# Feed-forward products by one level of a Strassen-type algorithm, in slots of half a product

## The chip, the cores and the metric

One core of a Trainium2 chip runs the kernel. The time is device microseconds of one execution, and the median of three runs is given. The core's engines work side by side and wait for each other by semaphores: TensorE (PE, matmuls into the banks of PSUM; its weight loads are PEld), VectorE (DVE), ScalarE (ACT), GpSimd (POOL) and SyncE (SP, which issues most loads and stores).

## What is computed

Two blocks follow each other on 1024 tokens of width 1024: the first has a gated linear attention and a pooling branch, the second has attention heads of two kinds and then a feed-forward part. The change is in the feed-forward part. All arithmetic is float32.

```python
x = x + o @ w_out[l]
h = rmsnorm_2(x, ffn_norm_g[l])
u = causal_dwconv(h @ w_up[l], conv_w[l], conv_b[l])   # three taps along the tokens
gate, val = jnp.split(u, 2, axis=-1)                   # 2816 columns each
x = x + (jax.nn.silu(gate) * val) @ w_down[l]
return rmsnorm_2(x, final_norm_g)
```

## The kernel before

Activations lie with features on the 128 partitions and 1024 tokens along the row, so x is 8 tiles, u is 44 tiles (22 gate, 22 value) and the feed-forward activations are NFF = 22 tiles. A product is exact to float32 by splitting both sides in two float32r parts, hi and lo, and doing three matmuls for one (`mm3`, lines 236 to 238: `ah*bl`, `al*bh`, `ah*bh`). A matmul is 128x128 weights against 512 tokens, one bank of PSUM. `gemm` does one tile of output columns, for the two halves of the tokens, over its k tiles.

Weights come in by `load` (line 227): a DMA of 256 KB on SP's queue to `wraw`, a cast on ScalarE to `whi` and a subtraction on GpSimd to `wlo`:

```python
nc.scalar.copy(hi, src)
tt(lo, src, hi.bitcast(F32), ALU.subtract, eng)   # eng is GpSimd, or VectorE if None
```

`tt` is a tensor_tensor operation (line 182), `stt` a scalar_tensor_tensor (line 185), both on VectorE if no engine is named.

The feed-forward part begins in the output projection of attention. For each of the 8 tiles of x2 (lines 1113 to 1126) VectorE scales the two halves out of PSUM (`t<-lg,rs`) and adds them (`x<-x,t`), ScalarE squares, GpSimd (for the last tile VectorE) adds the squares to `acc`, and the tile times the norm's weights is split to `u3h` (ScalarE) and `u3l` (VectorE). The first up product uses the first six tiles before the sums of squares are taken (`gemm_late`, line 1128). The factor of the norm, R3, is multiplied in as a product leaves PSUM (line 1143).

Then for each of 22 feed-forward tiles: an up product and convolution for the gate tile and the value tile (`conv`: one pass on ScalarE, two taps of `stt` on VectorE), a sigmoid, two products on VectorE, a split to `fh` and `fl`. For each two of them, `down` multiplies with the rows of w_down and adds to x2 out of PSUM (`x<-x,pp`). The order is that of the program as the framework's scheduler lays it out, and each next group's up products are traced ahead of the down products. The last two tiles and the final norm are done for some tokens at a time.

Tiles of the main pool are 32 slots of 1040 values, those of the weights 2 raw, 4 hi and 4 lo.

Of the kernel before, what the change touches and what calls it, by code (L numbers as in the profile page):

```python
# [9 lines left out]
F32 = mybir.dt.float32  # L10
# [7 lines left out]
P = 128  # L18
# [40 lines left out]
# columns of the vector table (one value per partition and column)  # L59
# [11 lines left out]
# columns of the constant table  # L71
# [7 lines left out]
# the first column tile of each block of w_mod  # L79
# [16 lines left out]
def fused_blocks(ctx, tc, io, out, dbg=None):  # L96
# [11 lines left out]
    wpool = ctx.enter_context(tc.tile_pool(name="wpool", bufs=1))  # L108
    sb = ctx.enter_context(tc.tile_pool(name="sb", bufs=1))
# [8 lines left out]

    def ld(name):
# [10 lines left out]
    def ht(name, dt=F32):  # L130
        return sb.tile([P, HALF], dt, tag="h", bufs=NH, name=f"{name}_{uid()}")
# [16 lines left out]
    # ---- constants  # L148
# [31 lines left out]
    # ---- arithmetic helpers  # L180
    def tt(o, a, b, op, eng=None):
        return (eng or nc.vector).tensor_tensor(out=o, in0=a, in1=b, op=op)  # L182

    def stt(o, a, s, b, op0, op1, eng=None):
        return (eng or nc.vector).scalar_tensor_tensor(out=o, in0=a, scalar=s, in1=b, op0=op0, op1=op1)  # L185

    def split(src, hi, lo, eng=None, scale=None):
        """src (times scale, one value per partition) = hi + lo exactly, both in float32r."""
        if scale is None:
            nc.scalar.copy(hi, src)  # L190
            tt(lo, src, hi.bitcast(F32), ALU.subtract, eng)
        else:
            nc.scalar.activation(hi, src, AF.Copy, scale=scale)
# [10 lines left out]
    def log_exp_table(after):  # L204
        """Loads the table that has both functions, past the last use of another."""
# [3 lines left out]
    def rstd(total, r, n, scale=1.0 / D):  # L209
        """r = 1 / sqrt(total * scale + eps): exp(-ln / 2), then one Newton step."""  # L210
# [9 lines left out]
    def sigmoid(src, o):  # L220
        """o = 1 / (1 + exp(-src)) as exp(-ln(1 + exp(-src)))."""
# [4 lines left out]
    # ---- products: weights are split into two float32r parts as they come in  # L226
# [15 lines left out]
    def gemm(parts, xh, xl, ranges=XH, c=P, c0=0, m=P, per=4, ks=range(KD), tag="pp"):  # L242
        """A tile of output columns; gives a bank of PSUM for each range of tokens."""
# [24 lines left out]
    def bank_rstd(acc, r, scale=1.0 / D, tag="pp"):  # L268
        """r = 1 / sqrt(mean + eps) from sums over all partitions of acc [128, 1024]."""
# [7 lines left out]
    def need(key):  # L277
        """Emits fillers up to the one called key."""
# [3 lines left out]
    def weave(fill, chain):  # L282
        """Emits each filler (key, step, function) before the given step of the chain."""
# [23 lines left out]
    x1_d = [dtile(f"x1_d{k}") for k in range(KD)]  # L307
    ra_d = dtile("ra_d")
# [7 lines left out]
    # ================================================================== block 1  # L316
# [3 lines left out]
    # conditioning vectors through silu  # L320
# [8 lines left out]
    # x and ctx (features first) and their norms  # L329
# [12 lines left out]
    # shift, scale (and later gate): the products with w_mod, 512 columns at a time, four tiles of  # L342
    # features side by side on the array; a second product sums the four and turns them to columns
# [63 lines left out]
    for b in range(2):  # L407
# [9 lines left out]
        for k in range(4 * b, 4 * b + 4):  # L417
# [4 lines left out]
            hl.append(b1k(f"hl{k}", F32R))  # L422
# [26 lines left out]
        # the gate inputs as [hi; lo; hi] on 96 partitions  # L449
# [30 lines left out]
    def proj_v(h):  # L480
        """v, token-major."""
# [16 lines left out]
    def proj_z(n, ct):  # L498
        """silu of the z parts, the sigmoid of the g parts, u itself."""
# [10 lines left out]
    # ---- gated linear attention of one head; yields between its steps  # L510
    def gla_head(h):
# [7 lines left out]
        # running sums of the log decays in each chunk (the 1/16 goes into the exponentials):  # L519
        # X[i] is the sum of the first i of the chunk  # L520
# [23 lines left out]
        # scores [key, query] of each chunk, by levels of halving: at each level the decays are  # L544
        # taken from the middle of the block, so that no exponent is above zero
# [60 lines left out]
        # queries against the states, decayed keys that build them  # L606
# [62 lines left out]
        # outputs, normed over the head  # L669
# [30 lines left out]
    def pool_tile(gi, i):  # L700
        """One tile of the pooled differences, in float32r parts."""
# [6 lines left out]
        # doubled window sums: s_w[t] covers t - w/2 .. t + w/2 - 1  # L708
# [71 lines left out]
    # branch products and the merge  # L780
# [17 lines left out]
    for ct in range(KD):  # L798
        sg, m = ld("sg"), b1k("mB")
# [26 lines left out]
    # residual; the two norms that follow it share their reads  # L826
    uh, ul = [], []
    accA, accB = b1k("accA"), b1k("accB")
    for ct in range(KD):
# [14 lines left out]
        ul.append(b1k("ul", F32R))  # L844
# [52 lines left out]
    def proj_v2(p):  # L897
        """v of two heads, turned to token-major."""
# [10 lines left out]
    def proj_f():  # L909
        """The running sums of the log forget gates, as rows [1, 1, F, -F, 1, 1] in parts."""  # L910
# [440 lines left out]
```

## Time and profile before

| | us |
|---|---|
| median of three runs | 2675.65 |
| lowest and highest run | 2673.03, 2675.9 |
| span of the profiled execution, first to last instruction | 2679.3 |

| engine | busy us | share of the span | instructions |
|---|---|---|---|
| PE | 2549.1 | 95% | 14390 |
| PEld | 2015.2 | 75% | 14390 |
| DVE | 1505.9 | 56% | 2190 |
| ACT | 961.0 | 36% | 1634 |
| POOL | 809.5 | 30% | 592 |

The profiled execution has no time of its own beside its span. Shares are means over all stages. Busy time of an engine holds the time in which an instruction that was begun could not go on. Matmuls overlap in their pipeline, so the mean duration of one is longer than their spacing; the spacing is a stretch of time divided by the matmuls in it.

### The profile page before, as it was taken

To read this page: it belongs to the slowest core of one execution; us is meant where nothing else is said; L and a number is where in the kernel's file an instruction comes from. 1 tells how busy PE (TensorE), PEld (TensorE's weight loads), DVE (VectorE), ACT (ScalarE), POOL (GpSimd) and SP (SyncE) were. 2 spreads that over 40 slices of the span, in tenths; PEclk is the share of its full clock that TensorE was granted. 3 is DMA by queue.
4 is the path that set the end of the run, shared out by engine and by line. 5 is a ranking of instruction groups with operands and counts; after the bars stand their busy time and mean duration, and the time that the engine had idled before them with its cause. 6 is when DMAs were issued, how large, how long until landed. Compare 5 with 4: busy or idle time off the path is not lost. (4 is left out here: it accounts for less than half of the span.)

```text
span 2679.3 us, 36279 instructions
## 1 busy us (share of the span) xinstructions
PE 2549.1 (95%) x14390; PEld 2015.2 (75%) x14390; DVE 1505.9 (56%) x2190; ACT 961.0 (36%) x1634; POOL 809.5 (30%) x592
## 2 busy tenths in 40 slices
PE   6989999999999999999999999999899999999996
PEld 3878977777787888876777766666688888888885
DVE  6363292765927223255766677788934444444456
ACT  4342262553734412332333443433422222222233
POOL 1432221221212224434233222233433333333334
PEclk9989999999999999999999999999999999999998
DMA  6423242433424553335444323430111111111112
GB/s 256 125 74 108 86 158 85 151 111 101 145 80 146 196 193 110 118 103 155 127 127 127 113 77 114 124 105 28 40 49 49 48 48 48 47 48 48 48 48 75
DMA packets 109113, 270.55 MB, mean 101 GB/s; under 512 B 13600, under 2 KB 18592, under 8 KB 108944
## 3 DMA queue, kind: packets, MB, share of 16 engines
q1 hardware_dynamic: 101648, 244.90, 28.3%
q0 software_dynamic: 7296, 23.34, 3.7%
q8 instruction: 113, 1.85, 0.3%
q14 instruction: 56, 0.46, 0.1%
HBM read 192.40 MB, written 71.57 MB: 99 GB/s over the span
## 5 line engine op out<-in xcount | busy, mean ns | idle before, releaser
L182 POOL TENSOR_TENSOR wlo<-wraw,whi 128x512 fp32r<-128x512 f32 (+1 forms) x363 | 537.3, 1482 | 1639.2 <-ACT whi L190 1593.1
L190 ACT CAST whi<-wraw 128x512 fp32r<-128x512 f32 (+1 forms) x363 | 223.8, 617 | 709.4 <-PE pp L238 617.6
L236 PE MATMUL pp<-hl,whi 128*128 128x512 f32 (+1 forms) x768 | 312.1, 407 | 4.8 <-DVE hl L185 4.8
L237 PE MATMUL pp<-hh,wlo 128*128 128x512 f32 (+1 forms) x768 | 307.2, 400 | 0.4 <-POOL wlo L182 0.4
L238 PE MATMUL pp<-hh,whi 128*128 128x512 f32 (+1 forms) x768 | 306.4, 399 | 0.0
L238 PE MATMUL pp<-u3h,whi 128*128 128x512 f32 x688 | 271.4, 395 | 0.0
L237 PE MATMUL pp<-u3h,wlo 128*128 128x512 f32 x688 | 271.0, 394 | 0.0
L236 PE MATMUL pp<-u3l,whi 128*128 128x512 f32 x688 | 270.2, 393 | 0.0
L182 DVE TENSOR_TENSOR x<-x,pp 128x512 f32<-128x512 f32 (+1 forms) x184 | 121.5, 664 | 208.5 <-PE pp L238 208.5
L236 PEld LDWEIGHTS pp<-hl,whi 128*128 128x128 f32 (+1 forms) x768 | 144.9, 189 | 42.5 <-DVE hl L185 5.8
L237 PEld LDWEIGHTS pp<-hh,wlo 128*128 128x128 f32 (+1 forms) x768 | 144.8, 189 | 38.9 <-issue 6.1
L238 PEld LDWEIGHTS pp<-hh,whi 128*128 128x128 f32 (+1 forms) x768 | 144.9, 189 | 33.7 <-issue 0.4
L1028 DVE COPY pt<-pg 128x512 f32<-128x512 f32 (+2 forms) x192 | 101.0, 553 | 92.5 <-PE pg L1026 91.8
L237 PEld LDWEIGHTS pp<-u3h,wlo 128*128 128x128 f32 x688 | 129.0, 188 | 30.9
L236 PEld LDWEIGHTS pp<-u3l,whi 128*128 128x128 f32 x688 | 129.2, 188 | 30.3
L238 PEld LDWEIGHTS pp<-u3h,whi 128*128 128x128 f32 x688 | 129.1, 188 | 30.1
L236 PE MATMUL pp<-fl,whi 128*128 128x512 f32 (+1 forms) x368 | 142.0, 386 | 0.0
L238 PE MATMUL pp<-fh,whi 128*128 128x512 f32 (+1 forms) x368 | 141.4, 384 | 0.0
L237 PE MATMUL pp<-fh,wlo 128*128 128x512 f32 (+1 forms) x368 | 140.8, 383 | 0.0
L185 DVE SCALAR_TENSOR_TENSOR t<-p,vec,t 128x1023 f32<-128x1023 f32 x88 | 122.1, 1395 | 33.1 <-ACT t L1144 32.1
L237 PE MATMUL pp<-uh,wlo 128*128 128x512 f32 x336 | 139.2, 414 | 0.0
L236 PE MATMUL pp<-ul,whi 128*128 128x512 f32 x336 | 138.3, 412 | 0.0
(384 smaller groups left out, 5434.0 us busy)
## 6 DMA issues: line engine op xcount, KB each, us to landing
wraw<-in_w_up SPq DMA_DIRECT2D x88, 256.0 KB
wraw<-in_w_qk SPq DMA_DIRECT2D x48, 256.0 KB
wm<-in_w_mod SPq DMA_DIRECT2D x24, 512.0 KB
wraw<-in_w_dn SPq DMA_DIRECT2D x44, 256.0 KB
x<-in_xT SPq DMA_DIRECT2D x16, 512.0 KB
wraw<-in_w_v SPq DMA_DIRECT2D x32, 256.0 KB
wraw<-in_w_out SPq DMA_DIRECT2D x32, 256.0 KB
q<-qs_d POOLq DMA_DIRECT2D x16, 512.0 KB, 5.0
```

The costliest lines, as they stand in the source:

```text
L182: return (eng or nc.vector).tensor_tensor(out=o, in0=a, in1=b, op=op)
L185: return (eng or nc.vector).scalar_tensor_tensor(out=o, in0=a, scalar=s, in1=b, op0=op0, op1=op1)
L190: nc.scalar.copy(hi, src)
L236: nc.tensor.matmul(ps, ah, bl, start=first, stop=False)
L237: nc.tensor.matmul(ps, al, bh, start=False, stop=False)
L238: nc.tensor.matmul(ps, ah, bh, start=False, stop=last)
L1028: nc.vector.tensor_copy(o, ps[:, :w])
```

## The change

The up product, for the gate tile q and the value tile q together, is a 2 by 2 matrix of quarters: output rows gate and value, token halves LOW and HIGH, features 0 to 3 and 4 to 7 as the inner dimension. Instead of 8 products of quarters it takes 7, of sums and differences of the quarters; a product n is 4 x 3 matmuls on one bank and is one slot. The sums of activations are made once (T, seven sets of four tiles in hi and lo, 56 tiles of 512), those of weights for each q (`up_sum`), and the results are combined as they leave PSUM (`up_result`): several products of a q accumulate in one bank, which is read between them. The factor of the norm is no longer multiplied in with the read of PSUM but by operations of its own (`scale` in `up_rest`: pg on VectorE, pv on GpSimd). The convolution and gating of q - 1 are spread over the seven slots of q.

The feed-forward tiles go to DRAM (`f_d`). The down product takes 20 of the 22 in three groups of 3, 3 and 4 pairs, again with 7 products for 8, the two tiles of a pair being the halves of the inner dimension; a slot is one n of one pair, 4 x 3 matmuls on four banks. The parts of a slot are made two slots ahead. The last two tiles are multiplied as before.

In the feed-forward part the instructions are kept in the order in which they are written (`pin`). The front's pools are closed and a new one laid over them. x2 is stored to DRAM and loaded again for the down results. The main pool has 24 slots and a pool `keep` has 8 (for hl, mB, ul, x1 and then pg, pv, the taps and x2). Comments were taken out. The core of the diff, lines that are only indented or moved left out:

```diff
-NSLOT, NF, NT, NLD, NH, NQT = 32, 3, 2, 3, 5, 5
+NSLOT, NKEEP, NF, NT, NLD, NQT = 24, 8, 3, 2, 3, 5
+N_T, N_RAW, N_SUM, N_W, N_E = 56, 8, 4, 9, 5
+DN_GROUPS = [
+    [(0, 3), (1, 4), (2, 5)], [(6, 9), (7, 10), (8, 11)], [(12, 16), (13, 17), (14, 18), (15, 19)],
+]
+SEVEN = (1, 6, 2, 5, 7, 3, 4)
+FIRST = (1, 2, 3, 7, 5, 6, 4)
...
-        u3h.append(b1k("u3h", F32R))
-        u3l.append(b1k("u3l", F32R))
-        split(x2[ct], u3h[ct], u3l[ct], None, V("ffg", ct))
-    R3 = b1k("R3")
-    u0, = gemm_late(
-        [[load(io["w_up"][0, j], 4, P) for j in range(2)]], u3h, u3l, tags=["lg"], k0=6, then=lambda: bank_rstd(acc, R3, tag="pg"),
-    )
+        nc.sync.dma_start(x2_d[ct], x1)
...
+        ps = get("pp")
+        nc.tensor.matmul(ps, ones, acc[:, a:b], start=True, stop=True)
+        total.append(ps)
+    front.close()
+    sb = ctx.enter_context(tc.tile_pool(name="ffn", bufs=1, reuse_waits="tile"))
+    pinned[0] = True
...
+    def t_parts(n, j):
+        b11, b12, b21, b22 = x2[j][:, LOW], x2[j][:, HIGH], x2[j + 4][:, LOW], x2[j + 4][:, HIGH]
+        eng = nc.gpsimd if j % 2 else None
+        if n in xq:
+            T[n].append(parts(xq[n][j], "t", None, V("ffg", j + 4 * (n > 1))))
+            return
+        if n == 7:
+            for k in (j, j + 4):
+                pin(nc.vector.tensor_scalar(x2[k], x2[k], V("ffg", k), None, op0=ALU.mult))
+            tt(b22, b22, b12, ALU.subtract)
+            src = b22
+        elif n == 5:
+            tt(b12, b12, b11, ALU.subtract)
+            src = b12
...
+        T[n].append(parts(src, "t", eng))
+    def up_sum(q, n):
+        a11, a12, a21, a22 = raws[q]
+        if n in (5, 6):
+            if (q, 5) not in sums_:
+                sums_[q, 5], sums_[q, 6] = seg("s1", "ws"), seg("s2", "ws")
+                tt(sums_[q, 5], a21, a22, ALU.add)
+                tt(sums_[q, 6], sums_[q, 5], a11, ALU.subtract)
+        elif n == 3:
...
+            tt(sums_[q, 3], a12, sums_[q, 6], ALU.subtract)
+        elif n == 7:
+            tt(a11, a11, a21, ALU.subtract)
...
+    def up_parts(q, n):
+        wh, wl = parts(sums_[q, n], "w", nc.gpsimd)
...
+    def up_product(q, n):
+        wh, wl = wparts.pop((q, n))
+        key = n if q == 0 else {1: 1, 2: 1, 7: 7, 4: 7}.get(n, 6)
...
+        for j in range(4):
+            th, tl = T[n][j]
+            mm3(ps, wh[:, j], wl[:, j], th, tl, j == 0 and n == key, j == 3, True)
+    def up_result(q, n):
+        b = lambda m: banks[q, m]
+        if n == 1:
+            part[q, 1] = seg("p1", "e")
+            pin(nc.scalar.copy(part[q, 1], b(1)))
...
+        elif n == 2:
+            pin(nc.scalar.copy(pg[:, LOW], b(2)))
+        elif n == 6:
+            part[q, 6] = seg("u", "e")
+            tt(part[q, 6], part[q, 1], b(6), ALU.add)
+        elif n == 4:
+            tt(pv[:, LOW], part[q, 6], b(4), ALU.add)
+        elif n == 5:
+            part[q, 5] = seg("v", "e")
+            tt(part[q, 5], part[q, 1], b(5), ALU.add)
+        elif n == 7:
+            tt(pv[:, HIGH], part[q, 5], b(7), ALU.add)
+        elif n == 3:
+            tt(pg[:, HIGH], part[q, 1], b(3), ALU.add)
+    def up_rest(q, i):
+        def tap(x, p_, k, ct):
+            stt(x[:, k:], p_[:, : L - k], V("cw", 44 * (2 - k) + ct), x[:, k:], ALU.mult, ALU.add)
+        def scale(p_, eng):
+            for half, r in zip((LOW, HIGH), R3):
+                tt(p_[:, half], p_[:, half], r, ALU.mult, eng)
...
+        if i == 0:
+            scale(pgv[q][0], None)
+            if q:
+                tg, tv = tiles.pop(q - 1)
+                tt(tg, tg, tv, ALU.mult)
+                dma(f_d[q - 1], tg)
+            return
...
+        if i == 1:
+            tiles[q] = [first(pg, q)]
+        elif i == 2:
+            tap(tiles[q][0], pg, 1, q)
+            scale(pv, nc.gpsimd)
+        elif i == 3:
+            tap(tiles[q][0], pg, 2, q)
+            tiles[q].append(first(pv, NFF + q))
+        elif i == 4:
+            g = act(pg, tiles[q][0], AF.Sigmoid)
+            tap(tiles[q][1], pv, 1, NFF + q)
...
+        elif i == 5:
+            tap(tiles[q][1], pv, 2, NFF + q)
+        else:
+            tt(tiles[q][0], tiles[q][0], pg, ALU.mult)
...
+    for s, (q, n) in enumerate(order):
+        i = s % 7
+        if s:
+            up_result(*order[s - 1])
+        if i == 0 and 0 < q < NFF - 1:
+            up_load(q + 1)
+        if i == 3 and q + 1 < NFF:
+            up_sum(q + 1, 6)
...
+        ahead(s + 2, up_parts)
+        if s + 2 < 7:
+            for j in range(4):
+                t_parts(order[s + 2][1], j)
+        if s == 2:
+            for ps in total:
+                R3.append(seg("R3", "R3"))
+                rstd(ps, R3[-1], HALF)
+        if q:
+            up_rest(q - 1, i)
+        up_product(q, n)
...
+        def sums(self, j):
+            q = self.q[j]
+            q["S1"], q["S2"], q["T3"], q["T2"] = (seg(n, "t") for n in ("S1", "S2", "T3", "T2"))
+            tt(q["S1"], q["A21"], q["A22"], ALU.add)
+            tt(q["S2"], q["S1"], q["A11"], ALU.subtract)
+            tt(q["T3"], q["B22"], q["B12"], ALU.subtract)
+            tt(q["T2"], q["T3"], q["B11"], ALU.add)
...
+            q[n] = parts(q[a], "w", nc.gpsimd), parts(q[b], "wr", nc.gpsimd if j % 2 else None)
...
+        if n == 5 and j == 0 and g + 1 < len(groups):
+            groups[g + 1].load(*EARLY, *REST)
+        prepare_sums(s + 3)
+        prepare(s + 2)
+        if late and s % 2 == 0:
+            o, p = late.pop(0)
+            tt(o, o, p, ALU.add, nc.gpsimd)
...
```

## Rows read from the trace of the kernel before

**Rows 1.** Busy time by stretch: stretch, us, engines (instructions), granted clock, DMA share, GB/s.

```profile
core 0: us, PE busy (x) PEld busy (x) DVE busy (x) ACT busy (x) POOL busy (x), PEclk, DMA share, GB/s
1905.50:1935.00 29.50, 21.08 (x72) 15.24 (x73) 26.91 (x26) 12.73 (x17) 16.25 (x7) 0.83 0.12 38
1946.60:2600.00 653.40, 653.40 (x2820) 529.02 (x2819) 313.61 (x348) 164.83 (x199) 210.31 (x139) 1.00 0.17 48
2000.00:2200.00 200.00, 200.00 (x864) 161.85 (x863) 96.52 (x108) 49.47 (x60) 63.55 (x42) 1.00 0.17 48
```

**Rows 2.** Order of time on POOL: start, us, instruction, idle before it.

```profile
2206.97 1.29 POOL L182 TENSOR_TENSOR wlo<-wraw,whi 128x512 fp32r<-128x512 f32 x1 [7.07 <-ACT whi L190]
```

**Rows 3.** Groups of 2000 to 2400 us: busy us, mean ns, idle before.

```profile
L182 POOL TENSOR_TENSOR wlo<-wraw,whi 128x512 fp32r<-128x512 f32 x72 | 98.6, 1369 | 243.0 <-ACT whi L190 243.0
...
L182 DVE TENSOR_TENSOR x<-x,pp 128x512 f32<-128x512 f32 x96 | 66.0, 688 | 129.9 <-PE pp L238 129.9
L190 ACT CAST whi<-wraw 128x512 fp32r<-128x512 f32 x72 | 44.7, 621 | 220.3 <-PE pp L238 220.3
...
L185 DVE SCALAR_TENSOR_TENSOR t<-p,vec,t 128x1023 f32<-128x1023 f32 x24 | 34.6, 1442 | 16.1 <-ACT t L1144 16.1
...
L1144 ACT ACTIVATE t<-p,vec 128x1024 f32<-128x1024 f32 x24 | 29.9, 1246 | 23.5 <-PE pp L236 22.4
...
L182 DVE TENSOR_TENSOR t<-t,sgf 128x1024 f32<-128x1024 f32 x12 | 14.7, 1225 | 1.1 <-ACT sgf L1166 1.0
...
L1166 ACT ACTIVATE sgf<-t 128x1024 f32<-128x1024 f32 x12 | 12.8, 1062 | 33.7 <-DVE t L185 33.7
```

**Rows 4.** Order of time on DVE, a tap that meets nothing.

```profile
2231.71 1.27 DVE L185 SCALAR_TENSOR_TENSOR t<-p,vec,t 128x1023 f32<-128x1023 f32 x1
```

**Rows 5.** Order of time on POOL, end of the output projection.

```profile
1908.79 1.74 POOL L182 TENSOR_TENSOR wlo<-wraw,whi 128x512 fp32r<-128x512 f32 x1
1910.68 3.21 POOL L182 TENSOR_TENSOR acc<-acc,sq 128x1024 f32<-128x1024 f32 x1
1913.84 2.28 POOL L182 TENSOR_TENSOR wlo<-wraw,whi 128x512 fp32r<-128x512 f32 x1
```

**Rows 6.** Order of time on DVE, the same stretch and what follows.

```profile
1905.92 3.46 DVE L182 TENSOR_TENSOR x<-x,t 128x512 f32<-128x512 f32 x2
1909.31 2.30 DVE L185 SCALAR_TENSOR_TENSOR u3l<-x,vec,u3h 128x1024 fp32r<-128x1024 f32 x1
1911.54 1.27 DVE L182 TENSOR_TENSOR t<-lg,rs 128x512 f32<-128x512 f32 x2
1912.73 2.23 DVE L185 SCALAR_TENSOR_TENSOR u3l<-x,vec,u3h 128x1024 fp32r<-128x1024 f32 x1
1914.89 2.37 DVE L182 TENSOR_TENSOR x<-x,t 128x512 f32<-128x512 f32 x2
...
1918.39 3.43 DVE L182 TENSOR_TENSOR x<-x,t 128x512 f32<-128x512 f32 x2
1921.74 1.27 DVE L185 SCALAR_TENSOR_TENSOR u3l<-x,vec,u3h 128x1024 fp32r<-128x1024 f32 x1
1923.07 1.22 DVE L182 TENSOR_TENSOR acc<-acc,sq 128x1024 f32<-128x1024 f32 x1
1924.21 1.28 DVE L185 SCALAR_TENSOR_TENSOR u3l<-x,vec,u3h 128x1024 fp32r<-128x1024 f32 x1
```

**Rows 7.** Groups of the whole span on DVE.

```profile
L185 DVE SCALAR_TENSOR_TENSOR u3l<-x,vec,u3h 128x1024 fp32r<-128x1024 f32 x8 | 14.4, 1797 | 0.2 <-ACT u3h L193 0.2
...
L978 DVE TENSOR_SCALAR pr<-pr,sm 128x1024 f32<-128x1024 f32 x8 | 6.0, 748 | 0.1
...
L182 DVE TENSOR_TENSOR osq<-osq 128x512 f32<-128x512 f32 x8 | 5.5, 693 | 39.1 <-ACT osq L685 39.1
```

**Rows 8.** Order of time on PE at the start of the feed-forward part.

```profile
1905.55 0.47 PE L236 MATMUL lg<-u3l,whi 128*128 128x512 f32 x1 [3.71 <-DVE t L182]
...
1924.35 3.52 PE L272 MATMUL pg<-acc,ones 128*128 128x512 f32 x4 [7.67 <-DVE acc L182]
...
1930.47 0.39 PE L236 MATMUL pp<-u3l,whi 128*128 128x512 f32 x1
```

**Rows 9.** The page's 40 slices: what the DMA engines moved.

```profile
GB/s 256 125 74 108 86 158 85 151 111 101 145 80 146 196 193 110 118 103 155 127 127 127 113 77 114 124 105 28 40 49 49 48 48 48 47 48 48 48 48 75
```

More of the change, by code (lines that the diff above doesn't have):

```diff
@@ L117, in b1k, with xk @@
         return bt(name, dt)[:, :L]
+    def xk(name, dt=F32):
+        return keep.tile([P, SLOT], dt, tag="x", bufs=NKEEP, name=f"{name}_{uid()}")[:, :L]
     def ld(name):
@@ L307, in fused_blocks @@
     x1_d = [dtile(f"x1_d{k}") for k in range(KD)]
+    x2_d = [dtile(f"x2_d{k}") for k in range(KD)]
+    f_d = [dtile(f"f_d{k}") for k in range(NFF)]
     ra_d = dtile("ra_d")
@@ L1110, in fused_blocks @@
     )
-    u3h, u3l = [], []
     acc = b1k("acc3")
@@ L1176, in down @@
-    def down(grp, wd, c2, fh, fl, ranges=XH):
-        for cc in range(2):
-            ct = 2 * c2 + cc
-            for ps, a, b in gemm([wd], fh, fl, ranges, c0=cc * P, per=2, ks=range(2)):
-                tt(x2[ct][:, a:b], x2[ct][:, a:b], ps, ALU.add)
-    def load_down(grp, c2):
-        return load(io["w_dn"][grp, c2], 2, DV)
-    f = up_group(0)
-    for grp in range(NFF // 2 - 1):
-        nf = up_group(grp + 1)
-        for c2 in range(4):
-            down(grp, load_down(grp, c2), c2, *f)
-        f = nf
@@ new lines, in fused_blocks @@
+    T = {n: [] for n in range(1, 8)}
+    xq = {n: [x2[j + 4 * (n in (2, 3))][:, HIGH if n == 3 else LOW] for j in range(4)] for n in (1, 2, 3)}
+    def t_parts(n, j):
[13 more added lines that the diff above has]
+        elif n == 6:
+            tt(b11, b22, b11, ALU.add)
+            src = b11
+        else:
+            tt(b21, b21, b11, ALU.subtract)
+            src = b21
+        T[n].append(parts(src, "t", eng))
@@ new lines, in last_gate, with ahead @@
+    def last_gate(q):
+        tg, tv = tiles.pop(q)
+        tt(tg, tg, tv, ALU.mult)
+        dma(f_d[q], tg)
+    order = [(q, n) for q in range(NFF) for n in (SEVEN if q else FIRST)]
+    def ahead(s, f):
+        if s < len(order):
+            f(*order[s])
+    up_load(0)
+    up_load(1)
+    for s in range(3):
+        up_sum(*order[s])
+    for s in range(2):
+        up_parts(*order[s])
+        for j in range(4):
+            t_parts(order[s][1], j)
+    for s, (q, n) in enumerate(order):
[6 more added lines that the diff above has]
+            up_sum(q + 1, 6)
+        if s + 3 < len(order) and order[s + 3][1] not in (5, 6):
+            up_sum(*order[s + 3])
+        elif s + 3 < len(order):
+            up_sum(*order[s + 3])
+        ahead(s + 2, up_parts)
+        if s + 2 < 7:
+            for j in range(4):
+                t_parts(order[s + 2][1], j)
[6 more added lines that the diff above has]
+        up_product(q, n)
@@ new lines, in fused_blocks, with result @@
+    groups = [Group(g) for g in DN_GROUPS]
+    steps = [(g, n, j) for g, gr in enumerate(groups) for n in SEVEN for j in range(len(gr.pairs))]
+    late = []
+    def result(g, n, c, ps):
+        if n == 1 and g == 0:
+            p1[c] = seg("p1", "e")
+            pin(nc.scalar.copy(p1[c], ps))
+        elif n == 1:
+            tt(p1[c], p1[c], ps, ALU.add)
+            if g == len(groups) - 1:
+                late.extend((x2[ct][:, half], p1[c]) for ct, half in ((c, HIGH), (c + 4, LOW), (c + 4, HIGH)))
+        else:
+            ct, half = {2: (c, LOW), 3: (c, HIGH), 5: (c + 4, HIGH), 7: (c + 4, HIGH), 4: (c + 4, LOW), 6: (c + 4, LOW)}[n]
+            o = x2[ct][:, half]
+            tt(o, o, ps, ALU.add)
@@ new lines, in fused_blocks, with prepare, prepare_sums @@
+    EARLY, REST = ("B11", "A11"), ("B12", "B22", "A21", "A22", "B21", "A12")
+    groups[0].load(*EARLY)
+    groups[0].load(*REST)
+    for ct in (4, 5, 6, 7):
+        x2_load(ct)
+    def prepare(s):
+        if s >= len(steps):
+            return
+        g, n, j = steps[s]
+        groups[g].parts(n, j)
+        if n == 6:
+            groups[g].sums2(j)
+        if n == 2:
+            groups[g].sums3(j)
+    def prepare_sums(s):
+        if s < len(steps) and steps[s][1] == 6:
+            groups[steps[s][0]].sums(steps[s][2])
@@ new lines, in fused_blocks @@
+    up_result(*order[-1])
+    for s in range(2):
+        prepare(s)
+    todo, al, be, ga = [], None, None, None
+    for s, (g, n, j) in enumerate(steps):
+        size = len(groups[g].pairs)
+        for _ in range(2):
+            if todo:
+                result(*todo.pop(0))
+        if s < 7:
+            up_rest(NFF - 1, s)
+        elif s == 7:
+            last_gate(NFF - 1)
+            for ct in range(4):
+                x2_load(ct)
+        if n == 5 and j == 0 and g + 1 < len(groups):
[5 more added lines that the diff above has]
+            tt(o, o, p, ALU.add, nc.gpsimd)
+        if j == 0 and n in (1, 6, 7):
+            new = [get("pp") for _ in range(4)]
+            al, be, ga = (new, be, ga) if n == 1 else (al, new, ga) if n == 6 else (al, be, new)
+        banks_ = {1: al, 2: al, 7: ga, 4: ga}.get(n, be)
+        (wh, wl), (th, tl) = groups[g].q[j].pop(n)
+        for c in range(4):
+            cs = slice(c * P, c * P + P)
+            mm3(banks_[c], wh[:, cs], wl[:, cs], th, tl, j == 0 and n in (1, 6, 7), j == size - 1, True)
+        if j == size - 1:
+            assert not todo
+            todo = [(g, n, c, banks_[c]) for c in range(4)]
@@ new lines, in fused_blocks, with raw_tile @@
+    while todo:
+        result(*todo.pop(0))
+    assert not late
+    pinned[0] = False
+    def raw_tile(name):
+        return seg(name, "t")
+    fl_, wl_ = {}, {}
+    for k in (NFF - 2, NFF - 1):
+        for h, half in enumerate((LOW, HIGH)):
+            f = raw_tile("f")
+            nc.sync.dma_start(f, f_d[k][:, half])
+            fl_[k, h] = parts(f, "t", None)
+            w = raw_tile("wl")
+            nc.sync.dma_start(w, io["w_dn"][k, h])
+            wl_[k, h] = parts(w, "t", nc.gpsimd)
@@ new lines, in fused_blocks, with in_half, last_down @@
+    rF = [raw_tile("rF") for _ in range(2)]
+    def in_half(a, b):
+        return a // HALF, slice(a % HALF, a % HALF + b - a)
+    def last_down(a, b):
+        h, ts = in_half(a, b)
+        for ct in range(KD):
+            cs = slice(ct % 4 * P, ct % 4 * P + P)
+            ps = get("pp")[:, : b - a]
+            for k in (NFF - 2, NFF - 1):
+                (wh, wl), (th, tl) = wl_[k, ct // 4], fl_[k, h]
+                mm3(ps, wh[:, cs], wl[:, cs], th[:, ts], tl[:, ts], k == NFF - 2, k == NFF - 1)
+            tt(x2[ct][:, a:b], x2[ct][:, a:b], ps, ALU.add)
@@ L1226, in fused_blocks @@
         a, b = RNG[n]
+        h, ts = in_half(a, b)
         if what == "product":
-            for c2 in range(4):
-                down(NFF // 2 - 1, wd[c2], c2, *f, [(a, b)])
+            last_down(a, b)
         elif what == "squares":
```

181 lines of the change are left out of this document (119 added, 62 removed).

## Prediction

> **What bounds the kernel now.** I read the page's head first, then the busy times by stretch. The span is 2679.3 us, 3.65 us above the median of the runs, 2675.65; I make the sum against the span and carry the difference to the median. In the feed-forward part the reader is to see a TensorE that never rests: between 1946.6 and 2600 us it is busy all 653.4 us at a granted clock of 1.00 (the level of 2.4 GHz), and in a middle stretch it does 864 matmuls in 200 us [rows 1], 0.2315 us each. VectorE is busy 96.5 of those 200 us, ScalarE 49.5, GpSimd 63.6. So before, a matmul less is 0.2315 us less, and everything else is cover. The question is how much of that cover is left.
>
> For that I went to the groups of the steady stretch and then to a crowded stretch ahead of it. GpSimd's `wlo` subtraction alone takes 1.29 us [rows 2], but 1.37 on average beside VectorE, and the taps (`t<-p,vec,t`) average 1.44 against 1.27 undisturbed [rows 3, 4]. The reason stands in the crowded stretch [rows 5, 6]. VectorE's two `x<-x,t` end at 1909.38; GpSimd's `wlo`, listed from 1908.79, ends at 1910.53, 1.15 later; VectorE's `u3l`, listed from 1909.31, ends at 1911.61, 1.08 after that; GpSimd's `acc` at 1913.89 (2.28 for 1024 columns); `u3l` at 1914.96 (1.07); `wlo` at 1916.12 (1.16); two adds at 1917.26 (0.57 each). From 1909.4 to 1917.3 these two engines take strict turns without a gap. The two `t<-lg,rs`, with one input in PSUM, run inside GpSimd's turn at 0.64 each. So a VectorE operation with two SBUF inputs and a GpSimd operation exclude each other; one with a PSUM input is free. I call the thing in dispute the port, and count how full it becomes.
>
> The Trainium skill, page "SBUF — State Buffer", section "Who interferes with whom", says the same: a VectorE instruction with two SBUF inputs and a GpSimd one that reads SBUF share a port pair as an exclusive lock, held for the whole instruction. The trace agrees on the exclusion; on "whole", a blocked `wlo` ends 1.15 us after its release where one alone lasts 1.29. This is the rule that speaks against the change.
>
> **TensorE.** Before: up 44 x 8 x 2 x 3 = 2112 matmuls, down 22 x 8 x 2 x 3 = 1056. After: up 22 x 7 x 12 = 1848, down 10 pairs x 7 x 12 = 840, and 96 for the two feed-forward tiles that stay classical. 384 fewer x 0.2315 = 88.9 us, if nothing else binds. A slot of 12 is 2.78 us; one q (a gate and a value tile) falls from 96 matmuls, 22.2 us, to 84, 19.45.
>
> **The up phase, q = 1 to 21.** Per q the port now carries, on GpSimd, seven `lo` parts and two halves of the scaling of pv, 9 operations of 512; on VectorE four sums of weights, two halves of the scaling of pg (6 of 512), four taps and two gate products (6 of 1024). With the turns of the crowded stretch: 9 x 1.15 + 6 x 0.57 + 6 x 1.08 = 20.3 us. With undisturbed durations (1.29; 0.69 for `osq` [rows 7]; 1.27; 1.22 [rows 3, 4]): 11.6 + 4.1 + 5.1 + 2.4 = 23.3. Either is above TensorE's 19.45: the port becomes the bound. VectorE's five results from PSUM (0.69 each [rows 3], 3.4) are free only where GpSimd happens to hold the port. The observed turns had no gap, so I take a value near the low end, 20.3 plus a fifth of 3.4: 21.0. That is 1.22 us less than 22.2, x 21 = -25.6 (bounds -40 and +23). ScalarE (7 casts of 0.62, two copies, two of 1.25, a sigmoid: about 9 us [rows 3]) has room.
>
> **q = 0 and the start.** Removed: the eight `u3l`, 14.4 us of VectorE ahead of the first product, six of them ahead of the last x2 tile [rows 6, 7]. Before, the products of k = 0 began at 1905.6 between these, rested up to 7.7 us at a clock of 0.83 [rows 1, 8], and the value tile's 48 matmuls follow from 1930.5, to 1941.6. After, no product comes ahead of the last x2 tile, since the sums of squares stand first in TensorE's queue and the parts T are made behind them. x2 is whole about 11 us earlier (six `u3l` at 1.08, four `wlo` of w_up at 1.15): 1911 instead of 1921.8. Then acc, 1.2; three sums and four parts of n = 1, 4: first product at 1916. From there the port has to make eight parts for n = 2 and 3 (8 x 0.57 = 4.6); n = 7: eight scalings of 1024 at 0.75 [rows 7], four sums, two parts on each engine, 11.7; n = 5, 6, 4: 5.7 each, 17.1; six weight parts, 6.9; the norm factor's three operations twice, 4.1; three sums, 1.7: 46.1 us, and the last product 2.8: 1964.9. Against 1941.6 that is +23. Bounds: +15 if the parts of n = 1 to 3 slip in ahead of the last x2 tiles, +33 at undisturbed durations and with the factor's waits for ScalarE bare.
>
> **Down.** Of the 10 pairs, 960 matmuls before, 222.2 us; after 840, 194.5. Port, by turns: a group of three pairs has 28 GpSimd (21 weight parts, 7 of the second pair's f) and 38 VectorE operations of 512: 53.9 us, under TensorE's 58.3. The first group also carries the last q's convolution, 9.9: 63.8. The group of four: 42 + 12 late additions on GpSimd, 46 on VectorE: 88.3 over TensorE's 77.8. Sum 63.8 + 58.3 + 88.3 = 210.4; with undisturbed durations 237. I take 213, near the turns: -9 (bounds -12, +15). The loads of the last group, 32 x 256 KB in the 12 slots between their issue and their group, want 250 GB/s; the fullest slice shows 256 [rows 9], and the first pairs' tiles are needed first, so I cost them at nothing; at the 158 of another slice they would end 20 us late.
>
> **Tail, and the rest.** The classical pair's parts come behind GpSimd's last pinned operation: four of 1.15, +4 (0 to 8). The norm behind it is as before. The stores of f and x2 and their reloads, about 31 MB over 750 us, add some 41 GB/s to 48 [rows 1]: hidden. In the front, 32 slots become 24 + 8 with the same tiles live: nothing; if a load waits for a slot, a few us.
>
> **Sum.** +23 - 25.6 - 9 + 4 = -7.6: span 2671.7, median 2668. Moving the norm factor (no longer in one operation with the PSUM read) is in it: the four scalings per q are port work that before was free.
>
> **Rivals.**
> *The results come late (slower).* Products 6, 5 and 3 of a q share a bank, 7 and 4 another, 1 and 2 a third. VectorE's result of slot s - 1 must be out before TensorE starts slot s + 1, within 2.78 - 0.69 = 2.1 us of slack; queued behind and ahead of it are taps and sums, each of which may first wait 1.15 for GpSimd. If GpSimd runs ahead and idles just while VectorE reads PSUM, all 3.4 us are exposed: 23.7 per q, +31; sum +49, median 2725. It decides from 21.4 us per q on, where the sum is zero. For it: slot 2 has 5.1 us of port work; against it: the parts are two slots ahead.
> *The lock holds whole instructions.* 23.3 per q, +23, down +15, start +33, tail +8: 2755. Against it: the 1.15 and 0.57 seen. This is what the skill's page makes of it, by its word "whole".
> *The port does not bind.* TensorE's count decides: 21 x -2.77 = -58, down -28, start +10: 2600. For it: nothing in the rows; it would need operations that overlap.
> *Nothing gained.* Start and turns cancel, 21.4 per q: 2676.
>
> **How the numbers follow.** Main case 0.55 (own range 2645 to 2690), late results 0.22, whole lock 0.05, no bind 0.10, cancelling 0.08. What a measurement tells from no change is 0.2%, 5.4 us. Faster: 0.36 of the main case and the 0.10; same: 0.11 and 0.08; slower: the rest. The range leaves out the 2600 and 2755 cases and takes in most of the late results: 2635 to 2715.
>
> **What would show it.** Right: in the up phase TensorE idles a little in every q at 21 us, VectorE and GpSimd operations with two SBUF inputs lengthened, their hold times summing to nearly the stretch; about 48 us from first product to the end of q = 0; the second down group at 58 us. Wrong: TensorE busy without rest (no bind), or its waits released by VectorE's PSUM results (late results), or a granted clock below 1.00 in the steady part, which I have not priced.

## The result, and the profile after

The changed kernel takes 2750.98 us (2747.74 to 2753.68) against 2674.86 of the kernel before on the same chip: ratio 1.0285, interval 1.0271 to 1.03. It is 2.85% slower. The forecast was 2668 with a range to 2715: wrong in sign, and outside the range.

The page of after: span, busy time of three engines, the granted clock in 40 slices, what the DMA engines moved.

```profile
span 2751.8 us, 36777 instructions
PE 2506.6 (91%) x14006; PEld 1972.4 (72%) x14006; DVE 1805.1 (66%) x2428; ACT 1054.9 (38%) x1849; POOL 1072.9 (39%) x758
...
PEclk9999999999999999999999999999799999999998
...
GB/s 249 126 76 106 109 132 78 154 112 147 93 91 189 229 121 95 130 95 162 128 129 121 94 87 124 150 26 103 27 69 69 69 69 69 69 146 207 58 20 61
```

The DMA engines move 69 GB/s in the steady part and 207 at most behind it, against 48 and 75 [rows 9]; TensorE waits for no load there. The page alone doesn't say where the time is. The busy times by stretch do, with the columns of [rows 1]: first q = 0, a steady stretch of the up phase, then the three down groups.

```profile
1924.00:1975.30 51.30, 32.28 (x84) 21.06 (x85) 46.81 (x59) 19.24 (x33) 22.38 (x14) 0.68 0.07 21
2000.00:2200.00 200.00, 178.11 (x733) 143.68 (x732) 173.95 (x149) 73.43 (x108) 127.91 (x79) 0.95 0.22 72
2455.00:2537.00 82.00, 64.48 (x253) 50.67 (x253) 64.63 (x70) 30.83 (x50) 47.33 (x32) 0.90 0.55 203
2537.00:2605.20 68.20, 59.73 (x253) 48.34 (x252) 52.05 (x67) 24.73 (x44) 39.90 (x28) 0.95 0.23 73
2605.20:2702.20 97.00, 82.36 (x337) 66.10 (x337) 73.11 (x78) 32.28 (x57) 81.04 (x54) 0.93 0.05 14
```

Before, 200 us held 864 matmuls, 200.00 busy, clock 1.00 [rows 1]; now they hold 733, TensorE rests for 21.9 of them, and the granted clock is 0.95, some matmuls at the level of 1.2 GHz. No engine is full: VectorE 174, GpSimd 128 of 200. So it is not an amount that binds; something is late.

Term by term, the spans differing by 72.5 us:

| part | forecast | measured | how |
|---|---|---|---|
| start and q = 0 | +23 | +33.7 | first product of q = 1 at 1975.3, before 1941.6 |
| up, q = 1 to 21 | -25.6 | +13.1 | 479.7, before 466.6 |
| down, ten pairs | -9 | +25.0 | 247.2 (82.0 + 68.2 + 97.0), before 222.2 |
| tail | +4 | +0.7 | what is left of the 72.5 |

Up and down are mixed in the kernel before; its 466.6 and 222.2 are worked out, from their matmuls at 0.2315 us each.

**Up.** What TensorE waited for from 1975 to 2455 us: us in total, times, longest.

```profile
PE pp L261 <- DVE v L206: 48.6, 20, 2.4
```

One rest in each q from 1 to 20, of 2.43 us, nearly always of the same length, ahead of product 3, ended by VectorE's `v`. That is the read of product 5 from the bank in which product 3 is to accumulate. (q = 21, in which no sums of a next q are made, has no such rest.) One such rest in TensorE's order of time, then what VectorE and GpSimd do meanwhile:

```profile
2219.17 0.39 PE L263 MATMUL pp<-hi,hi 128*128 128x512 f32 x1
2221.99 0.47 PE L261 MATMUL pp<-lo,hi 128*128 128x512 f32 x1 [2.43 <-DVE v L206]
```

```profile
2211.50 0.69 DVE L206 TENSOR_TENSOR u<-p,pp 128x512 f32<-128x512 f32 x1 [1.88 <-ACT hi L214]
2212.11 1.28 DVE L206 TENSOR_TENSOR s<-wr,s 128x512 f32<-128x512 f32 x1
2213.31 2.31 DVE L209 SCALAR_TENSOR_TENSOR t<-pg,vec,t 128x1023 f32<-128x1023 f32 x1
2215.54 1.78 DVE L206 TENSOR_TENSOR s<-wr,wr 128x512 f32<-128x512 f32 x1
2217.35 1.68 DVE L206 TENSOR_TENSOR s<-s,wr 128x512 f32<-128x512 f32 x1
2218.95 2.29 DVE L209 SCALAR_TENSOR_TENSOR t<-pg,vec,t 128x1022 f32<-128x1022 f32 x1
2221.17 0.68 DVE L206 TENSOR_TENSOR v<-p,pp 128x512 f32<-128x512 f32 x1
```

```profile
2211.54 1.29 POOL L206 TENSOR_TENSOR lo<-wr,hi 128x512 fp32r<-128x512 f32 x1 [0.30 <-ACT hi L214]
2212.80 3.97 POOL L206 TENSOR_TENSOR pv<-pv,R 128x512 f32<-128x512 f32 x2
2216.73 1.75 POOL L206 TENSOR_TENSOR lo<-s,hi 128x512 fp32r<-128x512 f32 x1
2218.69 1.48 POOL L206 TENSOR_TENSOR lo<-wr,hi 128x512 fp32r<-128x512 f32 x1 [0.21 <-POOL lo L206]
```

Between the two PSUM reads `u` and `v`, VectorE has a sum, a tap, two sums and a tap: five operations that undisturbed would be done in some 4.5 us. GpSimd's five stand against them in strict turns, and they take from 2212.1 to 2221.2, 9.1 us. A sum that ends at 2217.32 began at 2215.54, 1.78 long; its share of that is 0.6, the rest is GpSimd's hold. The groups of 2000 to 2400 us show the same as means (busy us, mean ns, idle before); undisturbed it is 1.27 and 0.69 [rows 4, 7]:

```profile
L209 DVE SCALAR_TENSOR_TENSOR t<-pg,vec,t 128x1023 f32<-128x1023 f32 (+1 forms) x35 | 80.6, 2302 | 0.0
...
L206 DVE TENSOR_TENSOR s<-wr,wr 128x512 f32<-128x512 f32 x18 | 32.0, 1777 | 0.0
...
L206 DVE TENSOR_TENSOR u<-p,pp 128x512 f32<-128x512 f32 x18 | 12.4, 688 | 32.2 <-ACT hi L214 32.2
```

The last row is the other side: VectorE stands idle 32.2 us in 18 q ahead of `u`. The profile names a cast of weights as what ended it, but product 6, which `u` reads, ends only 0.1 us before `u` starts (2211.39 and 2211.50), so VectorE could not have begun it sooner. VectorE has time to spare, in the wrong slots.

The q are of two lengths. In 15 of the 20 with the rest, six to eight matmuls soon behind it run at the level of 1.2 GHz, as here, and the q takes about 23.35 us; in the other five none does, and it takes 21.74.

```profile
2198.61 0.47 PE L261 MATMUL pp<-lo,hi 128*128 128x512 f32 x1 [2.45 <-DVE v L206]
...
2200.44 0.63 PE L261 MATMUL pp<-lo,hi 128*128 128x512 f32 x1
```

A q is 84 matmuls at the 0.2267 us of an undisturbed product, 19.04, and the rest, 2.43, and what the clock loses (1.6 in 15 of 20, a mean of 1.2): 22.7 of the 22.94 that a q takes on average.

**Down.** What TensorE waited for in the down groups:

```profile
PE pp L261 <- DVE lo L206: 36.5, 12, 7.6
PE pp L261 <- ACT p L1431: 3.4, 1, 3.4
PE pp L261 <- POOL lo L206: 2.1, 2, 1.2
```

Of these 42 us, 40 stand in the products n = 1, 6, 2 and 5, beside which the sums are made; in products 7, 3 and 4 TensorE hardly rests. The longest rest of the first group in TensorE's order of time, and the VectorE operations ahead of it:

```profile
2497.99 0.79 PE L261 MATMUL pp<-lo,hi 128*128 128x512 f32 x1 [7.13 <-DVE lo L206]
```

```profile
2488.25 2.32 DVE L209 SCALAR_TENSOR_TENSOR t<-pv,vec,t 128x1022 f32<-128x1022 f32 x1
2490.49 1.75 DVE L206 TENSOR_TENSOR S<-A,S 128x512 f32<-128x512 f32 x1
2492.16 1.74 DVE L206 TENSOR_TENSOR T<-B,T 128x512 f32<-128x512 f32 x1
2493.83 1.27 DVE L206 TENSOR_TENSOR x<-x,pp 128x512 f32<-128x512 f32 x2
2495.03 2.31 DVE L206 TENSOR_TENSOR t<-t,pg 128x1024 f32<-128x1024 f32 x1
2497.26 0.68 DVE L206 TENSOR_TENSOR lo<-B,hi 128x512 fp32r<-128x512 f32 x1
```

The part that TensorE needs stands behind sums for later products and the convolution of the last q, all but the two reads of PSUM (`x<-x,pp`) stretched by a turn of GpSimd.

**Start.** VectorE's first sum, and SyncE's issues ahead of it:

```profile
1920.12 0.69 DVE L206 TENSOR_TENSOR s<-wr,wr 128x512 f32<-128x512 f32 x1 [3.79 <-DMA wr<-in_w_up]
```

```profile
1885.73 28.48 SPq L1144 DMA_DIRECT2D x_d<-x  x8
1914.30 9.38 SPq L1183 DMA_DIRECT2D wr<-in_w_up  x9
```

SyncE issues the eight stores of x2, the last of which has to wait for the last x2 tile, and only then the first load of w_up. VectorE waits 3.79 us for it. Of the +33.7, 8 us are a first product at 1924.0 instead of the forecast 1916; q = 0 itself takes 51.3, forecast 48.9.

### The profile page after: what moved, and what is told of

Its sections match the earlier page's. It is cut to its first block, busy times and chain, and to the rows that moved or that the text cites. A ratio compares the mean times of both kernels' runs of the same rounds, so it can differ in the third digit from the quotient of the medians.

```text
span 2751.8 us, 36777 instructions
## 1 busy us (share of the span) xinstructions
PE 2506.6 (91%) x14006; PEld 1972.4 (72%) x14006; DVE 1805.1 (66%) x2428; ACT 1054.9 (38%) x1849; POOL 1072.9 (39%) x758
## 5 line engine op out<-in xcount | busy, mean ns | idle before, releaser
L206 POOL TENSOR_TENSOR wlo<-wraw,whi 128x512 fp32r<-128x512 f32 (+2 forms) x231 | 351.5, 1524 | 1253.7 <-ACT whi L214 1219.8
L261 PE MATMUL pp<-lo,hi 128*128 128x512 f32 (+1 forms) x944 | 388.2, 411 | 113.2 <-DVE v L206 48.6
L262 PE MATMUL pp<-hi,lo 128*128 128x512 f32 (+1 forms) x944 | 382.2, 405 | 0.4 <-POOL lo L206 0.3
L263 PE MATMUL pp<-hi,hi 128*128 128x512 f32 (+1 forms) x944 | 381.3, 404 | 0.0
L261 PEld LDWEIGHTS pp<-lo,hi 128*128 128x128 f32 x944 | 187.9, 199 | 173.3 <-issue 56.7
L214 ACT CAST whi<-wraw 128x512 fp32r<-128x512 f32 (+2 forms) x231 | 141.9, 615 | 333.5 <-PE pp L263 259.7
L262 PEld LDWEIGHTS pp<-hi,lo 128*128 128x128 f32 x944 | 188.5, 200 | 39.9 <-POOL lo L206 2.0
L263 PEld LDWEIGHTS pp<-hi,hi 128*128 128x128 f32 x944 | 188.0, 199 | 40.2
L263 PE MATMUL pp<-uh,whi 128*128 128x512 f32 x336 | 135.3, 403 | 0.0
L263 PE MATMUL pp<-rh,whi 128*128 128x512 f32 x320 | 127.3, 398 | 0.0
```

The costliest lines, as they stand in the source:

```text
L206: return pin((eng or nc.vector).tensor_tensor(out=o, in0=a, in1=b, op=op))
L214: pin(nc.scalar.copy(hi, src))
L261: pin(nc.tensor.matmul(ps, ah, bl, start=first, stop=False, skip_group_check=again))
L262: pin(nc.tensor.matmul(ps, al, bh, start=False, stop=False, skip_group_check=again))
L263: pin(nc.tensor.matmul(ps, ah, bh, start=False, stop=last, skip_group_check=again))
```

## The experiments

Two theories ran through them. 'Order' (in some expectations 'bursts'): a read or a part comes late because of what stands ahead of it in VectorE's queue, so it matters where work stands, not how much there is. 'Port' (or 'total', 'turns'): what matters is what VectorE and GpSimd take from each other. All ratios are to the kernel before on the same chip.

**own_bank.** Product 3 gets a bank, so that `v` need not be out before it starts.

```diff
-key = ... {1: 1, 2: 1, 7: 7, 4: 7}.get(n, 6)
+key = ... {1: 1, 2: 1, 7: 7, 4: 7, 3: 3}.get(n, 6)
-            tt(pg[:, HIGH], part[q, 1], b(3), ALU.add)
+            tt(pg[:, HIGH], part[q, 5], b(3), ALU.add)
```

> Edit: product n = 3 gets a bank of its own and no longer adds to the bank of 6 and 5; same operations otherwise. Theory 'order' (TensorE waits 2.43 us in every q because VectorE's read of product 5 stands behind a burst of sums and taps, while product 3 wants the same bank; the clock loss of about 1.2 us per q follows from that rest): the rest goes, the clock in the up phase is 1.00, a q falls from 22.96 to 20.3 or less, the time to 2698 or below. Theory 'total' (the port's work of 20.3 to 23.3 us per q is the bound): the wait only moves to another product, a q stays at 21.7 or more, the time at 2725 or more.

2713.02, ratio 1.0131 (1.0108 to 1.0155). A q takes 20.95 us instead of 22.94; the clock is back at 1.00, VectorE full:

```profile
2000.00:2200.00 200.00, 186.34 (x799) 148.05 (x798) 199.66 (x163) 79.39 (x114) 160.84 (x88) 1.00 0.23 75
```

A smaller rest opens ahead of product 4 (1.23 us, ended by `pv`, the read of product 7). So the shared bank cost 2.0 us a q, some 1.2 of it by the clock. 'Order' was right on the rest and the clock and too hopeful on the time: what is left, 20.95, is the 21.0 that the prediction had for the port, with VectorE busy, its waits for turns included, all the time. (The spans of the two profiled executions differ by 44.0 us; 6.5 of that are not of this edit: the first product came at 1917.5 instead of 1924.0.)

**sums_slot5.** The early sums S5 and S6, which stand ahead of `v`, are made two slots later.

```diff
-        if i == 3 and q + 1 < NFF:
-            up_sum(q + 1, 6)
```

> Edit: the two sums of weights for the next q move from slot 3 to slot 5; same operations, same banks. 'Order': the read of product 5 comes 2 x 0.57 + 2 x 1.15 = 3.4 us earlier, the rest of 2.43 us goes, a q falls to 20.3 or less, the time to 2698 or below. 'Total': the same port work, so within 10 us of 2751.

2721.62, ratio 1.0161 (1.0136 to 1.0185); a q takes 21.4 in all but the first two, the rest at product 3 is gone, the clock 1.00:

```profile
2000.00:2200.00 200.00, 185.65 (x791) 146.71 (x790) 182.57 (x160) 77.74 (x111) 150.14 (x84) 1.00 0.24 78
```

The same work in another place gives back 1.5 us a q: more than 'total' allowed, but not down to the 20.3 of 'order'. Smaller rests (1.2 on a GpSimd part, 0.4 on a cast) come up at product 5, whose sums are now the late thing.

**slack_work.** Two needless multiplications a q into a tile that is no longer read, in slot 6.

```diff
             tt(tiles[q][0], tiles[q][0], pg, ALU.mult)
+            for half in (LOW, HIGH):
+                tt(pg[:, half], R3[0], R3[1], ALU.mult)
```

> Edit: two more VectorE products of two SBUF inputs (512 columns each, 1.14 us of port per q) in slot 6 of each q, into a tile that is dead by then. 'Order': they fall where VectorE waits for TensorE (1.2 + 0.5 + 1.9 us in a q), so the time stays within 5 us of 2751. 'Total': 21 x 1.14 = 24 us more, 2775.

2759.81, ratio 1.0309 (1.0284 to 1.0334); a q takes 23.12, 0.18 more for two operations that hold the port 1.14. The whole up phase takes 487.6 us instead of 479.7, so 7.9 of the 24 of 'total'. The time is 8.8 above that of the changed kernel, a little outside the 5 of 'order', but far nearer to it: in the changed kernel the amount of port work counts for a third at most.

**up_vector.** On top of the own bank, all nine GpSimd operations of a q go to VectorE, which seemed full.

```diff
-        wh, wl = parts(sums_[q, n], "w", nc.gpsimd)
+        wh, wl = parts(sums_[q, n], "w", None)
-            scale(pv, nc.gpsimd)
+            scale(pv, None)
```

> Edit: the kernel with a bank of its own for product 3, and in the up phase the nine operations per q that ran on GpSimd (seven lo parts, two halves of the scaling of pv) now on VectorE; GpSimd has nothing there. In own_bank VectorE is busy 199.7 of 200 us, a q is 20.95. Theory 'port' (most of that busy time is waiting for GpSimd's turns: own work 13.3, the rest turns of 1.15; an operation moved costs 0.57 and takes away 1.15): VectorE's work is 18.4 us per q, TensorE binds at 84 x 0.2267 = 19.0, a q is 19.0 to 19.8, the time 18 to 30 us under own_bank, 2683 to 2695. Theory 'VectorE is overloaded' (its busy time is its own work): nine more operations of 0.69 make a q 27 us, the time 2830.

2676.75, ratio 0.9998 (0.9988 to 1.0008); a q takes 19.29:

```profile
2000.00:2200.00 200.00, 200.00 (x877) 163.49 (x876) 199.66 (x273) 87.51 (x127) 0.00 (x0) 1.00 0.27 86
```

VectorE is busy 199.66 us in both kernels, with 163 instructions beside GpSimd's 88 and with 273 alone. Alone, operations of 512 start 0.60 apart: 20 x 0.60 and six of 1024 at 1.19 are 19.1, as much as TensorE's 84 matmuls. GpSimd's help cost more than it took off; 'port' is right of what binds once the order is mended, and had even put the gain too low (its 2683 at best). The Trainium skill, page "SBUF — State Buffer", section "Who interferes with whom", calls the port pair that VectorE and GpSimd share an exclusive lock. This run fits that, with 1.66 us a q gained by leaving the second holder idle.

**down_later, down_spread, down_ahead.** The sums of the down phase, moved: later by one product (A21 - A11 and the like beside n = 2, S and T beside n = 7); the same, and the first four sums 9 steps ahead instead of 3; parts three steps ahead instead of two.

```diff
-        if n == 6:
-            groups[g].sums2(j)
         if n == 2:
-            groups[g].sums3(j)
+            groups[g].sums2(j)
+        if n == 7:
+            groups[g].sums3(j)
```

> Edit in the down phase alone: the second and third sets of sums of a pair are made when they are next needed (behind the parts of products 2 and 7) instead of behind 6 and 2; same operations. 'Order' (the 42 us of rest in the down phase stand at products 1, 6 and 2 because the sums are made there at once): the rests there shrink by a third to a half, the time by 15 to 25 us, to about 2731. 'Total' (VectorE's and GpSimd's work per group is the bound): within 5 us of 2751.

2742.01, ratio 1.024 (1.0218 to 1.0262): rests 35.5 instead of 42.0, groups 81.8, 64.7, 94.1, together 240.6. 'Order' had 15 to 25 us; the time fell by 9. For scale: in the seven kernels whose down phase is written as in the changed one, it takes 244.9 to 250.9 us.

> Edit in the down phase alone: down_later, and the first sums of a pair nine steps ahead of their product instead of three, so that those of the second and third group fall into the quiet products 3 and 4 of the group before (for the first group they stand ahead of its first step). Same operations. 'Order': the rests of groups two and three at products 6 and 2 go, groups of about 59 and 84 to 88 us instead of 68 and 97, the time about 25 us under the changed kernel, 2726. 'Total': no more than down_later's 10 us.

2742.54, ratio 1.0253 (1.0238 to 1.0268): groups 88.3, 63.3, 85.6, together 237.2. Against down_later the second and third gain 1.4 and 8.5; the first loses 6.5 of that, where its sums now stand ahead of its first step (a rest of 7.2 us in product 1, 3.1 in down_later). In total it is no better than down_later, as 'total' had it; in the third group 'order' was right.

> Edit in the down phase alone: parts are made three steps ahead instead of two, sums four instead of three; the rings of parts hold four pairs, so no more memory. 'Order': a step of 2.7 us more to absorb the burst takes 2.7 us off each of the larger rests, about 10 us in all, 2740. 'Total': no change.

2747.02, ratio 1.0269 (1.0252 to 1.0286): groups 81.5, 69.0, 96.3, together 246.9, inside the 244.9 to 250.9 of kernels without the edit. The rests fall from 42.0 to 37.6, but no gain in time is shown: lead doesn't shorten a queue that every step's part stands in.

**down_vector.** The lo parts of the down phase on VectorE.

```diff
-... parts(q[a], "w", nc.gpsimd), parts(q[b], "wr", nc.gpsimd if j % 2 else None)
+... parts(q[a], "w", None), parts(q[b], "wr", None)
```

> The changed kernel, with all 14 lo parts of a pair in the down phase on VectorE (before: ten or eleven on GpSimd); the twelve late additions stay on GpSimd. 'turns' (it is GpSimd's holds that make the sums of a step late, and VectorE has the time): VectorE has 66 operations of 0.685 us with SBUF inputs and 28 reads of PSUM of 0.68 in a group of three, 64 us; 74 with the last q's convolution; 79 to 90 for the group of four: down 219 to 230 instead of 247.2, median 2723 to 2734, the longest rests (7.1, 5.5, 7.6 us) less than halved. 'bursts' (what counts is how many operations stand ahead of a step's parts in VectorE's queue): two to three more in each slot, the rests at n = 6 and 2 stay or grow, down 247 or more, median 2751 or more.

2729.12, ratio 1.0201 (1.0186 to 1.0216): groups 75.1, 63.2, 87.4, together 225.7 instead of 247.2, rests 26.1. 'Turns' had 219 to 230. But a rest of 7.0 us stays in the last group at n = 6, where 'turns' had the longest halved. GpSimd is not out of it there: its late additions fall on the four sums ahead of the part.

```profile
2606.83 6.30 POOL L206 TENSOR_TENSOR x<-x,p 128x512 f32<-128x512 f32 x4 [153.87 <-DVE p L206]
```

```profile
2610.26 1.75 DVE L206 TENSOR_TENSOR T<-B,B 128x512 f32<-128x512 f32 x1
```

The four sums take from 2607.2 to 2613.6, 6.4 us; the same four ahead of them took 2.7 (2600.95 to 2603.61). So by estimate 3.7 of the 7.0 are turns again, and what is left may be the order; a run without the late additions there was not made.

**start_stores, start_order.** The last two stores of x2 issued behind the first loads of w_up; the sums of activations of q = 0 made ahead of their parts.

```diff
-        nc.sync.dma_start(x2_d[ct], x1)
+        if ct < KD - 2:
+            nc.sync.dma_start(x2_d[ct], x1)
...
     up_load(0)
+    for ct in (KD - 2, KD - 1):
+        dma(x2_d[ct], x2[ct])
```

> Edit at the start alone: the stores of the last two tiles of x2 stand behind the first four loads of w_up in SyncE's queue, which otherwise wait behind the store of the last tile. Theory 'queue': the loads land before x2 is whole, VectorE's wait of 3.8 us for them goes, from the sums of squares to the first product 3.9 us instead of 7.7, the time 3 to 5 us less. Theory 'parts': the parts are what is late, no change.

2749.0, ratio 1.0278 (1.0262 to 1.0293). VectorE's wait for the load is gone, and the first product follows the end of acc by 4.8 us instead of 7.7 ('queue' had 3.9); of the whole that is too little to be told from nothing.

> The changed kernel, with the four sums of activations of a product of q = 0 (n = 7, 5, 6, 4) made ahead of the four pairs of parts, where each pair came right behind its sum. 'order' (VectorE's lo waits 0.7 to 1.2 us for ScalarE's cast of the sum just made, twice a product): q = 0 takes 44 us instead of 51.3, median 2743. 'amount' (the port's 46 us of work and TensorE at its lower clock set it, not the order): 50 to 52, median 2749 to 2752.

2747.6, ratio 1.0272 (1.0257 to 1.0287): q = 0 takes 50.8 instead of 51.3. 'Amount' was right for this kernel.

**all_reordered, mixed_reordered.** All of it together (down_ahead left out, the longer lead of the sums only for the second and third group); then the same with the weight parts of products 7, 3 and 4 of the down phase on GpSimd again.

> All at once: the own bank, the up parts and the scaling of pv on VectorE, the last stores of x2 behind the first loads of w_up, the sums of q = 0 ahead of their parts, the down lo parts on VectorE, the later down sums one product later and those of the second and third group nine steps ahead. If the gains add up: 2676.75 of the kernel with the up phase on VectorE, less 2 (stores), 7 (order of q = 0), 17 to 28 (down lo parts), 4 (later sums): 2636 to 2647. If 'bursts' is right for the down phase: 2664 or more. If the lost time comes back elsewhere (a rest removed in one place opens in the next): about 2670.

2640.47, ratio 0.9871 (0.9857 to 0.9886): the gains add up. The stretches of q = 0, up and the three groups:

```profile
1919.90:1967.30 47.40, 25.43 (x86) 17.73 (x86) 46.86 (x63) 20.45 (x36) 19.98 (x8) 0.78 0.08 22
2000.00:2200.00 200.00, 200.00 (x876) 163.36 (x875) 199.65 (x271) 86.25 (x125) 0.00 (x0) 1.00 0.26 81
2374.00:2450.20 76.20, 63.79 (x253) 48.74 (x253) 71.75 (x111) 31.53 (x52) 0.00 (x0) 0.96 0.65 238
2450.20:2510.80 60.60, 57.58 (x253) 47.03 (x251) 59.27 (x98) 25.40 (x45) 0.00 (x0) 1.00 0.21 66
2510.80:2594.10 83.30, 80.13 (x337) 65.36 (x338) 71.65 (x105) 30.38 (x54) 37.96 (x16) 0.96 0.06 16
```

Up is 406.8 (before 466.6), down 220.1 (before 222.2); q = 0 is 47.4. Neither GpSimd out of its weight parts alone (51.3 in up_vector) nor the other order alone (50.8), nor the moved stores alone (51.3 in start_stores), gave that; together they did, and no run says why. Of the gain that 384 matmuls less could bring, the most is now lost at the start (q = 1 begins 25.7 us later than before) and in the first down group: 252 matmuls at 0.2280 are 57.5 us, it takes 76.2, and VectorE is busy 71.75 of them.

> The kernel with all at once, but with the lo parts of w_dn for n = 7, 3 and 4 on GpSimd, three of a pair's 14. VectorE then has 28.3 operations of 0.685 us a pair, 19.4, against TensorE's 84 matmuls, 19.0 to 19.2. 'turns': each of the three holds the port 1.15 us, in which VectorE can read PSUM: 19.4 + 3.5 - 2 = 20.8 us a pair against 21.4 with all on VectorE: 6 us less than that kernel. 'amount of GpSimd work costs more than it takes off': 5 us more.

2642.95, ratio 0.9877 (0.986 to 0.9893). Three of 14 parts back on GpSimd neither gain 6 us nor cost 5; neither figure was right, and where VectorE is close to full the two choices come out alike.

## Why the prediction was wrong

**The step that failed is the up phase**, "I take a value near the low end, 20.3 plus a fifth of 3.4: 21.0", and with it the weight on the main case. The sum of the port's work was good: with product 3 in its own bank a q takes 20.95 and q = 1 to 21 take 440.7, 25.9 less than before, where the sum had 25.6 (that it is so near is in part luck, since the fifth was a guess). What the sum left out is that a mean binds only if TensorE can run ahead. Three products in one bank tie each start to a read two products back, and the read of product 5 stands behind five operations that the turns stretch to 9.1 us. That is the rival *the results come late*, held at 0.22: its cause and its releaser were right. Its price, 23.7 a q against 22.94, came near by other pieces: it added exposed reads of PSUM to the port's 20.3, where in fact a rest of 2.43 and the clock stand on TensorE's own 19.04. It named slot 2 with 5.1 us of port work against two slots of room; following one q through VectorE's queue in order, each operation at its turn, would have shown `v` late. It has been shown by two edits that leave the amount alone: another bank, and other places for two sums. Of the 80.1 us between forecast and measured span, up is 38.7, down 34.0, the start 10.7, the tail -3.3.

**The clock** was left unpriced. With a rest of 2.43 us in each q the granted clock was 0.95: it fell behind 15 of the 20 rests, at 1.6 us each, 24 us. Without the rest it is 1.00.

**Down** failed in the same way, and no rival had parts late there: 213 was a mean of turns, 247.2 was measured, with 42 us of rests where the sums are crowded and 0.90 to 0.95 of the clock. Moving sums gave 7 to 10 us of this back, more lead nothing that can be told from the spread of that phase, taking GpSimd's parts out 21.5.

**The start** was mis-sized by 10.7 (bound +33, measured +33.7): the eight stores in SyncE's queue ahead of the loads were not followed; moving two of them gave 2.9 back. About 3.7 came from the front, whose last product of the output projection ends at 1905.55 instead of 1901.85. That end lies between 1898.2 and 1907.3 over the changed kernels of this study, whose front up to there is the same, and the first product between 1913.8 and 1925.4; why the front moves stays open. q = 0 itself was 2.4 over. **The tail**, +0.7 for +4, was inside its bounds.

**The turns** of 1.15 and 0.57 us, read in the trace before, hold: in the down stretch VectorE's `S<-A,S` and `T<-B,T` end 1.66 apart (2492.24 and 2493.90), about one turn of GpSimd and one of their own (1.72). *The lock holds whole instructions* came near in the total (2755) by another way; 20.95 with the own bank speaks against its 23.3.

## What to carry to other kernels

When a change takes work from the bound engine and gives it to others, a sum of their work per period is only the lower bound: follow one period through the fullest queue in order and ask for each read that frees a bank when it is out. Reads that free PSUM belong ahead of work that nobody waits for, and products whose results are read in between need a bank each. Before giving GpSimd elementwise work beside a VectorE that reads two SBUF inputs, count its hold: here VectorE alone did in 19.29 us what both did in 20.95.

## What was not expected of the hardware

- VectorE's busy time contains its waits for turns: 199.66 of 200 us with 163 instructions and with 273. A full engine in the profile may be one that waits.
- A product of 12 matmuls takes 2.72 us in the changed kernel, 0.2267 each, against 0.2315 before [rows 1]; with VectorE alone 877 in 200 us, 0.2280. No run separates the cause.
- With rests of 2.43 us, one in 23, the granted clock was 0.95, and it fell behind 15 of 20 of them; with rests of 1.2 us, one in 21, it was 1.00.
